# Moving 156 DMA issues of a hybrid encoder block from the sync queue to GpSimd's queue

## The chip, the cores and the metric

The kernel runs on one core of one Trainium2 chip. The core has five instruction streams that run side by side, each in its own order: TensorE (PE, with its weight loads as PEld), VectorE (DVE), ScalarE (ACT), GpSimd (POOL) and SyncE (SP). They wait for one another by semaphores. A DMA is an instruction on the stream that issues it; it waits there for its operands, and what stands behind it on that stream waits too. The metric is the device time of one execution in microseconds (us); lower is better.

## The reference, cut to what matters

One layer over 1040 tokens (16 meta tokens and 1024 frames) of width 1024, all in float32:

```
h = h + token_mixer(rmsnorm(h))          # proj = u @ w_in ; 4 mLSTM heads and 4 retention heads
h = h + channel_mixer(rmsnorm(h))        # (silu(conv(u @ w_up)) * (u @ w_gate)) @ w_down
return rmsnorm(h)[meta tokens dropped]

token_mixer:   q, k, v, gates = split(proj)
               h_head = chunkwise recurrence(q, k, v)          # per head
               mixed  = sigmoid or silu(gate) * head_norm(h_head)
               return mixed @ w_out
```

`mixed` has 2048 features: 8 heads of 256. `w_out` is 2048 x 1024, `w_down` is 2816 x 1024.

## The kernel before, in words

Activations lie transposed, features on the 128 partitions and tokens along the free axis. Each fp32 product is made of three products of halves (`hi` and `lo` of both sides), so each weight tile is loaded raw (`raw_*`, two buffers of a ring in all), then split: `hi` by ACT (L142) and `lo` by DVE (L143).

The token mixer goes head by head, h = 0 to 7. In a head, PE makes the gate projection `po` (L376 to L378) between the first chunks of the recurrence, then the value projection `pv` of the next head (L366 to L368) between the later chunks, then q and k of the next head (`pq`, `pk`). DVE evacuates `pq` and `pk` from three PSUM banks: L397 for mLSTM heads, L407 to L410 for retention heads. The finished features of a head, `mixed`, are made by DVE in tiles `mx` (L896, two buffers) and stored to DRAM, `mxd` (L908): six stores a head for heads 0 to 6, 42 in all. Head 7 stays on the chip.

The products with `w_out` and `w_down` come later and use a scheme of seven products in place of eight, which needs sums and differences of blocks of these weights. They are made ahead of time, one `wsum` at a time, in the evacuations of q and k: 8 for `w_out` (`wsw`) and 11 for `w_down` (`wsd`), 19 in all. One `wsum` loads two tiles of 128 x 1024 (L182, L183), combines them in place by four DVE instructions (L185 to L188) and stores four halves of 128 x 512 (L190). There is one buffer for each of its two tiles (`rr0`, `rr1`), so the loads of the next `wsum` wait until the stores of the last have landed. Three `wsum` stand in each of six heads and one in another. So twelve of them follow another in the same head.

Two more parts matter here. `last_two` (L169, L172) loads rows of `w_out` into the same ring of raw tiles, and DVE adds them into `acc` when a head's last piece of `mixed` is there; the raw tile is free after that, and the next head's `raw_v` goes into it. `tables` (L520, L521) loads rows of the gates, spread over all partitions, into `A1` and `A2`.

The order of each engine's instructions is set when the kernel is built, by a scheduler that simulates the program with costs of its own; DMA issues count there too. So an edit of a queue moves instructions on other engines as well. Before, SP issues all DMAs but one of ACT's, and POOL does little but memsets.

Of the kernel before, what the change touches and what calls it, by code (L numbers as in the profile page):

```python
# [30 lines left out]
HB = 4 * P  # L31
# [30 lines left out]
def body(ctx, tc, h_in, vecs, cst, mask_in, rot, w_v0, w_v, w_fm, w_out, w_up, w_gate, w_down, out):  # L62
    nc = tc.nc
# [9 lines left out]
    def after(later, first):  # L73

        tc.add_manual_dep(later.ins, first.ins.name, mybir.DependencyInfo(mybir.DependencyClass.NoSync, mybir.DependencyReason.DATA),
                          reason="order")
# [17 lines left out]
    mxd = [dram.tile([P, SEQ], F32, name=f"mxd{i}") for i in range(16)]  # L94
# [82 lines left out]
    sums = {(g, st, k): dram.tile([P, 2 * HB], F32, name=f"ws{g}{st}_{k}") for g, n in (("w", 8), ("d", KD)) for st in ("65", "73") for k in range(n)}  # L177

    def wsum(g, k):
        src, n = (w_out, 8) if g == "w" else (w_down, KD)  # L180
        a, b = (accp.tile([P, 2 * HB], F32, tag=f"rr{i}", name=f"ws{g}{k}_{i}") for i in range(2))
        nc.sync.dma_start(a, src[k])  # L182
        nc.sync.dma_start(b, src[k + n])  # L183
        w11, w21, w12, w22 = a[:, :HB], a[:, HB:], b[:, :HB], b[:, HB:]
        after(nc.vector.tensor_tensor(w22, w21, w22, ALU.add), last["qk"])  # L185
        nc.vector.tensor_tensor(w21, w21, w11, ALU.subtract)
        nc.vector.tensor_tensor(w11, w22, w11, ALU.subtract)
        nc.vector.tensor_tensor(w12, w12, w11, ALU.subtract)  # L188
        for st, i, x in (("65", 0, w11), ("65", 1, w22), ("73", 0, w12), ("73", 1, w21)):
            nc.sync.dma_start(sums[g, st, k][:, i * HB:(i + 1) * HB], x)  # L190

    wsums = [(g, k) for g, n in (("w", 8), ("d", KD)) for k in range(n)]

# [74 lines left out]
    def gained(kb, t0, t1, gcol, dve=False):  # L268
        g = vec[:, gcol + kb:gcol + kb + 1]
        if dve:  # L270
            nc.vector.tensor_scalar(uh[kb][:, t0:t1], resid[:, kb, t0:t1], g, None, ALU.mult)
        else:
            nc.scalar.activation(uh[kb][:, t0:t1], resid[:, kb, t0:t1], AF.Copy, scale=g)
        return nc.vector.scalar_tensor_tensor(ul[kb][:, t0:t1], resid[:, kb, t0:t1], g, uh[kb][:, t0:t1].bitcast(F32), ALU.mult, ALU.subtract)
# [33 lines left out]
    st = mix.enter_context(tc.tile_pool(name="st", bufs=1))  # L308
# [6 lines left out]
    def sig(b, p):  # L315
        t0, t1, _ = PIECES[p]
        return sigs[1][:, b] if p == 2 else sigs[0][:, b, max(t0, KEEP) - KEEP:t1 - KEEP]
# [387 lines left out]
    MA, MB = KEEP, KEEP + HALF  # L705
    wslots = {}

    def wact(q, k):
        i = ("A1", "B1", "B2", "A2").index(q) * 2 + k // 4
        if i not in wslots:  # L710
            wslots[i] = upool.tile([P, 2 * T], F32, tag=f"u{'hl'[i % 2]}{i // 2}", name=f"wa{i}")
        x = wslots[i][:, k % 4 * HB:(k % 4 + 1) * HB]
        mixw.act[q, k] = x
        return x
# [145 lines left out]
    def post_steps(h, p):  # L860
        t0, t1, chs = PIECES[p]
        n = len(chs)
        m = {}

        def stats():
            num, mv, base = outs.pop(p)
            z = mxp.tile([P, 4], F32, tag="z", name=f"z{h}_{p}", bufs=2)
            if h < H:
                den = base[:, 0:n, DV]
                e2 = cols[:, 2].rearrange("p (c h) -> p h c", h=H)[:, h, chs[0]:chs[0] + n]  # L870
                nc.vector.tensor_tensor(z[:, :n], den, den, ALU.mult)
                nc.vector.tensor_tensor(z[:, :n], z[:, :n], e2, ALU.max)
                nc.vector.scalar_tensor_tensor(z[:, :n], z[:, :n], EPS, mv[:, 0:n, 1], ALU.mult, ALU.add)
                nc.scalar.activation(z[:, :n], z[:, :n], AF.Sqrt)
            else:
                nc.scalar.activation(z[:, :n], mv[:, 0:n, 1], AF.Sqrt, bias=cs[:, C_EPS + h - H:C_EPS + h - H + 1])
            nc.vector.reciprocal(z[:, :n], z[:, :n])
            nc.vector.scalar_tensor_tensor(mv[:, 0:n, 1], mv[:, 0:n, 0], -1.0, z[:, :n], ALU.mult, ALU.mult)
            for i, c in enumerate(chs):
                L = CH[c][1]  # L880
                nc.scalar.activation(num[i][:L, :DV], num[i][:L, :DV], AF.Identity, bias=mv[:L, i, 1:2], scale=z[:L, i:i + 1])
            m["num"] = num

        def half(b):
            num = m["num"]
            tr = ps.tile([P, 512], F32, tag="tr", name=f"tr{h}_{p}_{b}")
            for i, c in enumerate(chs):
                c0, L = CH[c]
                nc.tensor.transpose(tr[:, c0 - t0:c0 - t0 + L], num[i][:L, b * P:(b + 1) * P], ident[:L, :L])
            a0 = max(t0, KEEP)  # L890
            w = t1 - a0
            g = (V_MLG if h < H else V_RTG) + (h % H) * 2 + b
            i = 2 * h + b

            def mix_into(dst, x0, x1):
                nc.vector.scalar_tensor_tensor(dst, tr[:, x0 - t0:x1 - t0], vec[:, g:g + 1], sig(b, p)[:, x0 - a0:x1 - a0], ALU.mult, ALU.mult)  # L896
            if h == 7:
                for q, o in (("A2", MA), ("B2", MB)):
                    x0, x1 = max(a0, o), min(t1, o + HB)
                    if x0 < x1:  # L900
                        mix_into(wact(q, 6 + b)[:, x0 - o:x1 - o], x0, x1)
                if t1 > MB + HB:
                    mix_into(mm[:, i], MB + HB, t1)
                return
            mx = mxp.tile([P, WMAX], F32, tag="mx", name=f"mx{h}_{p}_{b}", bufs=2)
            mix_into(mx[:, :w], a0, t1)
            e = min(t1, MB + HB)
            nc.sync.dma_start(mxd[i][:, a0 - MA:e - MA], mx[:, :e - a0])  # L908
            if e < t1:
                nc.vector.tensor_copy(mm[:, i], mx[:, e - a0:w])  # L910
        return [stats, lambda: half(0), lambda: half(1)]

    def ab(h, c):
# [47 lines left out]
    for i, (t0, t1) in enumerate(NP):  # L961
        for kb in range(KB):
            x = gained(kb, t0, t1, V_MIX, dve=kb < 4 if i == 0 else i > 1 and kb % 4 == 0)
# [19 lines left out]
    for h in range(8):  # L983
        A = lambda c, h=h: (lambda: scan_a(h, c))
        B = lambda c, h=h: ab(h, c)
        merge([lambda b=b, p=p: o_group(h, b, p) for b in range(2) for p in range(3)],
              [A(0)] + [B(c) for c in range(4 if h < 7 else NCH)])
        if h == 7:
            break
        side = post_steps(h, 0) + [B(4), B(5), B(6)] + post_steps(h, 1) + [B(7), B(8)] + post_steps(h, 2)  # L990
        merge([lambda c=c: v_group(h + 1, c)() for c in range(NCH)], side)
        tables(h + 1)
        for kind in "qk":
            for p in range(3):
                qk_group(h + 1, kind, p)
                if (kind, p) in (("q", 0), ("q", 2), ("k", 1)) and wsums:
                    wsum(*wsums.pop(0))
# [141 lines left out]
    for t, (st, k) in enumerate(mixw.steps):  # L1139
# [4 lines left out]
        if st == "65" and k == 1:  # L1144
            x = fp.tile([P, 4 * XW], F32, name="wm", tag="xh2", bufs=1)
# [175 lines left out]
    def up_part(i):  # L1321
        chunks = UC
        def done(m, half, c):
            if isinstance(c, list):
                t = ftile(f"c{i}_{m}{half}")
                for x, (j0, j1) in zip(c, chunks):
                    nc.scalar.copy(t[:, j0:j1], x)
                c = t
            conv(i, m, half, c)
        return seven("up", i, chunks, done)  # L1330

    def gate_part(i):
        def done(m, half, c):
            gate(i, m, half, c[0] if isinstance(c, list) else c[:, :HALF])
        return seven("ga", i, [(2, XW)], done)
# [50 lines left out]
    for i in range(1, NPAIR):  # L1386
        u, g = up_part(i), gate_part(i)
# [100 lines left out]
    for p in (1, 2):  # L1488
# [5 lines left out]
        else:  # L1494
            for mb in (1, 4):
                x = resid[:, mb, OP[2][0]:OP[2][1]]
# [84 lines left out]
```

## Time and profile before

| | us |
|---|---|
| median of 3 runs (1546.46 to 1555.4) | 1554.75 |
| the profiled execution, its own time | 1551.87 |
| its span | 1550.1 |
| PE busy in the span | 1515.9 |
| DVE busy in the span | 1123.7 |

The span runs from the first to the last instruction. A busy share is an average over stages; which wait ends last in a stage is read from the rows of that stage. A bracket at the end of a row of the timeline is the idle time of the engine ahead of that row and who ended it. "issue" there means that the engine waited for nothing that the profile shows. SPq is SP's queue of DMA issues, and the time of an SPq row is that of the issue, not of the transfer. Of the median's three runs one was at 1546.46 and one at 1555.4; the profiled execution lies between.

### The profile page before, as it was taken

Reading aid. Unit: us, or ns where it says so; the run is one execution under the profiler, and the core shown is the slowest. Engines: PE = TensorE matmul, PEld = TensorE weight load, DVE = VectorE, ACT = ScalarE, POOL = GpSimd, SP = SyncE. Lnnn points to the kernel's source line nnn. Section 1 sums busy time; section 2 is a strip of 40 time slices with the busy share of each in tenths; the row PEclk is TensorE's granted clock in tenths of the full one; section 3 lists DMA queues with packets and bytes.
Section 4 is the critical chain, followed back from the end, with each engine's and each line's share of the span. In section 5 each row is a group of like instructions: output and inputs, shape, how many; then the busy total and the mean of one; then the engine's idle time right before and its main releaser. Section 6 shows DMA issues by size and latency. Waiting matters only on the chain.

```text
span 1550.1 us, 25404 instructions
## 1 busy us (share of the span) xinstructions
PE 1515.9 (98%) x9753; PEld 1392.7 (90%) x9753; DVE 1123.7 (72%) x2387; ACT 737.0 (48%) x1493; POOL 2.4 (0%) x12
## 2 busy tenths in 40 slices
PE   7999999999999999999999999999999999999997
PEld 7989999999999999997788998999999999888887
DVE  8757768596767767679967778676666666778657
ACT  8574655545242433436454455444444444434443
POOL 0000000000000000000000000000000000000000
PEclk9999999999999999999999999999999999999999
DMA  6125435262534435227543235332222224933313
GB/s 214 42 70 168 158 106 182 86 225 96 179 116 149 146 116 171 88 84 250 177 137 108 82 96 177 102 98 87 82 82 79 79 82 148 374 98 114 95 41 109
DMA packets 92441, 197.41 MB, mean 127 GB/s; under 512 B 9048, under 2 KB 31264, under 8 KB 92320
## 3 DMA queue, kind: packets, MB, share of 16 engines
q1 hardware_dynamic: 92176, 195.73, 38.2%
q8 instruction: 76, 1.25, 0.3%
q14 instruction: 45, 0.37, 0.1%
q10 hardware_dynamic: 144, 0.07, 0.0%
HBM read 146.44 MB, written 49.32 MB: 126 GB/s over the span
## 4 chain that ended last, share of the span: by engine, by line
PE 85%; DMA 7%; DVE 4%; ACT 2%; issue 2%; SPq 0%; DVEq 0%; ACTq 0%
PE pv L366 4%; PE pv L367 4%; PE pv L368 3%; PE pdx L546 3%; PE pdx L548 3%; PE pdx L547 3%; PE po L378 3%; PE po L376 3%; PE po L377 3%; PE pup_x L547 2%; PE pup_x L548 2%; PE pga_x L546 2%; PE pup_x L546 2%; PE pga_x L548 2%; PE pga_x L547 2%; DMA A<-scr 2%
## 5 line engine op out<-in xcount | busy, mean ns | idle before, releaser
L366 PE MATMUL pv<-hi_v,uh 128*128 128x256 f32 (+1 forms) x512 | 146.5, 287 | 12.4 <-ACT hi_v L142 8.1
L367 PE MATMUL pv<-lo_v,uh 128*128 128x256 f32 (+1 forms) x512 | 145.7, 285 | 0.0
L368 PE MATMUL pv<-hi_v,ul 128*128 128x256 f32 (+1 forms) x512 | 144.9, 284 | 0.0
L376 PE MATMUL po<-uh,hi_o 128*128 128x386 f32 (+2 forms) x384 | 125.1, 326 | 0.0
L377 PE MATMUL po<-ul,hi_o 128*128 128x386 f32 (+2 forms) x384 | 123.3, 321 | 0.0
L378 PE MATMUL po<-uh,lo_o 128*128 128x386 f32 (+2 forms) x384 | 122.9, 320 | 0.0
L366 PEld LDWEIGHTS pv<-hi_v,uh 128*128 128x128 f32 x512 | 97.1, 190 | 15.9 <-ACT hi_v L142 8.1
L367 PEld LDWEIGHTS pv<-lo_v,uh 128*128 128x128 f32 x512 | 96.8, 189 | 0.9 <-DVE lo_v L143 0.8
L368 PEld LDWEIGHTS pv<-hi_v,ul 128*128 128x128 f32 x512 | 96.7, 189 | 0.1
L235 ACT CAST hi_up<-raw_up 128x512 fp32r<-128x512 f32 (+1 forms) x52 | 36.5, 720 | 108.5 <-PE pga_z L547 61.2
L376 PEld LDWEIGHTS po<-uh,hi_o 128*128 128x128 f32 x384 | 72.5, 189 | 0.2
L377 PEld LDWEIGHTS po<-ul,hi_o 128*128 128x128 f32 x384 | 72.4, 188 | 0.2
L378 PEld LDWEIGHTS po<-uh,lo_o 128*128 128x128 f32 x384 | 72.3, 188 | 0.1
L236 DVE TENSOR_TENSOR lo_ga<-fraw_ga,hi_ga 128x512 fp32r<-128x512 f32 (+1 forms) x52 | 41.8, 808 | 37.0 <-ACT hi_ga L235 36.9
L546 PE MATMUL pup_x<-uh_g,hi_up 128*128 128x256 f32 (+1 forms) x240 | 67.3, 283 | 1.2 <-ACT uh_g L1014 1.2
L547 PE MATMUL pup_x<-ul_g,hi_up 128*128 128x256 f32 (+1 forms) x240 | 67.5, 283 | 0.1
L236 DVE TENSOR_TENSOR lo_up<-raw_up,hi_up 128x512 fp32r<-128x512 f32 (+1 forms) x52 | 41.2, 809 | 35.0 <-ACT hi_up L235 34.2
L548 PE MATMUL pup_x<-uh_g,lo_up 128*128 128x256 f32 (+1 forms) x240 | 66.3, 282 | 0.0
L376 PE MATMUL pq<-uh,hi_q 128*128 128x400 f32 (+2 forms) x192 | 63.1, 328 | 1.7 <-DVE vl L342 1.6
L376 PE MATMUL pk<-uh,hi_k 128*128 128x400 f32 (+2 forms) x192 | 62.3, 324 | 2.0 <-DVE kT L409 1.5
L236 DVE TENSOR_TENSOR lo_d<-rd,hi_d 128x1024 fp32r<-128x1024 f32 (+1 forms) x34 | 37.6, 1112 | 34.0 <-ACT hi_d L235 34.0
L377 PE MATMUL pq<-ul,hi_q 128*128 128x400 f32 (+2 forms) x192 | 62.1, 323 | 0.0
(744 smaller groups left out, 4981.6 us busy)
## 6 DMA issues: line engine op xcount, KB each, us to landing
wsd<-w_down_d SPq DMA_DIRECT2D x22, 512.0 KB, 4.1
wsd<-wsd SPq DMA_DIRECT2D x44, 256.0 KB, 2.1
raw_up<-w_up_d SPq DMA_DIRECT2D x22, 512.0 KB, 3.6
fraw_ga<-w_gate_d SPq DMA_DIRECT2D x22, 512.0 KB, 3.6
acts<-cv SPq DMA_DIRECT2D x44, 256.0 KB, 2.0
rd<-wsd SPq DMA_DIRECT2D x22, 512.0 KB, 3.4
wsw<-w_out_d SPq DMA_DIRECT2D x16, 512.0 KB, 4.3
raw_o<-w_fm_d SPq DMA_DIRECT2D x16, 512.0 KB, 3.5
```

Source lines behind the costliest of these rows:

```text
L235: nc.scalar.copy(hi[:, o:o + n], x)
L236: nc.vector.tensor_tensor(lo[:, o:o + n], x, hi[:, o:o + n].bitcast(F32), ALU.subtract)
L366: nc.tensor.matmul(pv[:L, :nv], a, hi[:, o:o + nv], start=kb == 0, stop=False)
L367: nc.tensor.matmul(pv[:L, :nv], a, lo[:, o:o + nv], start=False, stop=False)
L368: nc.tensor.matmul(pv[:L, :nv], b, hi[:, o:o + nv], start=False, stop=kb == KB - 1)
L376: nc.tensor.matmul(pt[:, :n], a, uh[kb][:, t0:t1], start=kb == 0, stop=False)
L377: nc.tensor.matmul(pt[:, :n], a, ul[kb][:, t0:t1], start=False, stop=False)
L378: nc.tensor.matmul(pt[:, :n], b, uh[kb][:, t0:t1], start=False, stop=kb == KB - 1)
L546: m.append(nc.tensor.matmul(pt, ah, xh_, start=first and k == 0, stop=False, skip_group_check=True))
L547: nc.tensor.matmul(pt, ah, xl_, start=False, stop=False, skip_group_check=True)
L548: m.append(nc.tensor.matmul(pt, al, xh_, start=False, stop=last and k == n - 1, skip_group_check=True))
```

## The change

The two loads and four stores of each `wsum`, and the stores of `mx`, are issued from GpSimd's queue in place of SP's. SP keeps the loads of weights and tables, and the transfers of the later stages. That is 19 x 6 + 42 = 156 DMAs: SP has 348 rows in place of 504, POOL 172 in place of 16.

```
@@ wsum
-        nc.sync.dma_start(a, src[k])
-        nc.sync.dma_start(b, src[k + n])
+        nc.gpsimd.dma_start(a, src[k])
+        nc.gpsimd.dma_start(b, src[k + n])
...
         for st, i, x in (("65", 0, w11), ("65", 1, w22), ("73", 0, w12), ("73", 1, w21)):
-            nc.sync.dma_start(sums[g, st, k][:, i * HB:(i + 1) * HB], x)
+            nc.gpsimd.dma_start(sums[g, st, k][:, i * HB:(i + 1) * HB], x)
@@ post_steps, half
-            nc.sync.dma_start(mxd[i][:, a0 - MA:e - MA], mx[:, :e - a0])
+            nc.gpsimd.dma_start(mxd[i][:, a0 - MA:e - MA], mx[:, :e - a0])
```

SP's queue at the start of the program, before (`resid` is the input, `raw_q` and `raw_k` the first head's weights):

```order
L937 DMA resid<-h_in_d 128x8x384
L937 DMA resid<-h_in_d 128x8x256
L182 DMA wsw_0_1802<-w_out_d 128x1024
L183 DMA wsw_1_1803<-w_out_d 128x1024
L139 DMA raw_q_0_223<-w_fm_d 128x1024
L139 DMA raw_k_0_618<-w_fm_d 128x1024
```

and POOL's queue at the start, now:

```order
L332 MEMSET vh 128x258
L333 MEMSET vl 128x258
L182 DMA wsw_0_1802<-w_out_d 128x1024
L183 DMA wsw_1_1803<-w_out_d 128x1024
L334 MEMSET vh 128x9x2
L335 MEMSET vl 128x9x2
L336 MEMSET vh 128x9
L908 DMA mxd_94<-mx_0_0_1325 128x386
```

The first pair of `wsum` loads stood behind all loads of the input; it stands now behind two memsets at the very start and waits for nothing there.

DVE at the evacuation of k of head 4, with the second `wsum` of that stretch (`wsd_1_5191`, `wsd_0_5190`); one piece of the difference, `-` before, `+` now:

```order
-L185 TENSOR_TENSOR wsd_1_5191<-wsd_0_5190,wsd_1_5191 128x512
 L858 BN_AGGR mv_2_4962<-bn_7_4981 128x2
 L831 MEMSET mv_0_5426 128x2
-L186 TENSOR_TENSOR wsd_0_5190<-wsd_0_5190 128x512
 L407 TENSOR_TENSOR rk_0_5233<-pk_0_5208,A_173 64x400
 L408 TENSOR_TENSOR rk_0_5233<-pk_0_5208,A_173 64x400
 L409 TENSOR_TENSOR kT<-pk_0_5208,A_172 128x400
-L187 TENSOR_TENSOR wsd_0_5190<-wsd_1_5191,wsd_0_5190 128x512
 L342 SCALAR_TENSOR_TENSOR vl<-pv_8_5031,Rg,vh 128x256
 L774 TENSOR_TENSOR qd_2l<-qT,qd_2h 128x128
```

The evacuation of the first bank of k (L407 to L409) no longer stands behind L185, which waits for the two loads; L185 stands now twelve rows on, behind L410 of that bank.

SP's queue where head 1 ends and the weights of head 2 are loaded, now:

```order
L139 DMA raw_o_1_1894<-w_fm_d 128x1024
L169 DMA raw_m_2014<-w_out_d 128x1024
L169 DMA raw_m_2153<-w_out_d 128x1024
L520 DMA A_172<-scr 128x16
L139 DMA raw_v_0_2358<-w_v_d 128x1024
L139 DMA raw_v_1_2364<-w_v_d 128x1024
L139 DMA raw_q_0_2370<-w_fm_d 128x1024
```

Before, 22 DMAs of `wsum` and `mx` stood between the first and the last of these rows, and `raw_v` stood right behind a pair of `wsum` loads.

## Rows read from the trace of the kernel before

**Rows 1.** The page: busy time, share and instructions of each engine.
```profile
PE 1515.9 (98%) x9753; PEld 1392.7 (90%) x9753; DVE 1123.7 (72%) x2387; ACT 737.0 (48%) x1493; POOL 2.4 (0%) x12
```

**Rows 2.** The page: shares by engine of the chain that ended last.
```profile
PE 85%; DMA 7%; DVE 4%; ACT 2%; issue 2%; SPq 0%; DVEq 0%; ACTq 0%
```

**Rows 3.** Windows: stretch, busy time per engine, granted clock, DMA share, GB/s.
```profile
0.00:50.00 50.00, 41.54 (x301) 39.19 (x302) 41.56 (x112) 34.49 (x83) 1.03 (x10) 1.00 0.54 187
50.00:200.00 150.00, 144.39 (x1043) 139.33 (x1042) 108.01 (x322) 93.63 (x192) 0.00 (x0) 1.00 0.33 106
200.00:450.00 250.00, 243.51 (x1748) 235.02 (x1747) 187.22 (x490) 115.91 (x257) 0.00 (x0) 1.00 0.46 149
450.00:700.00 250.00, 250.00 (x1840) 246.39 (x1840) 178.53 (x445) 100.53 (x245) 0.00 (x0) 1.00 0.38 123
2.00:20.00 18.00, 11.87 (x84) 10.32 (x85) 15.28 (x41) 14.21 (x38) 0.00 (x0) 1.00 1.05 370
```

**Rows 4.** Timeline of SP's queue at the start: start, issue time, operation, count.
```profile
0.74 0.99 SPq L103 DMA_DIRECT2D resid<-h_in_d  x2
1.78 1.92 SPq L139 DMA_DIRECT2D raw_v<-w_v_d  x4
...
9.27 2.97 SPq L182 DMA_DIRECT2D wsw<-w_out_d  x1
12.28 0.44 SPq L183 DMA_DIRECT2D wsw<-w_out_d  x1
```

**Rows 5.** Timeline of PE: its first row, and one in head 4.
```profile
8.13 0.59 PE L366 MATMUL pv<-hi_v,uh 128*128 128x264 f32 x1 [8.13 <-ACT hi_v L142]
...
413.09 0.39 PE L376 MATMUL pk<-uh,hi_k 128*128 128x256 f32 x1 [1.51 <-DVE kT L409]
```

**Rows 6.** Timeline of DVE ahead of that row of head 4.
```profile
409.84 0.69 DVE L185 TENSOR_TENSOR wsd<-wsd,wsd 128x512 f32<-128x512 f32 x1 [3.92 <-issue]
...
411.29 0.58 DVE L407 TENSOR_TENSOR rk<-pk,A 64x400 f32<-64x400 f32 x1
411.88 0.57 DVE L408 TENSOR_TENSOR rk<-pk,A 64x400 f32<-64x400 f32 x1
412.46 0.57 DVE L409 TENSOR_TENSOR kT<-pk,A 128x400 f32<-128x400 f32 x1
...
414.54 0.57 DVE L410 TENSOR_TENSOR kT<-kT,rk 128x400 f32<-128x400 f32 x1
```

**Rows 7.** The chain in order of time, from one wsum of head 2 to the next.
```profile
227.85 0.69 DVE wsw L188
228.56 2.16 DMA wsw<-wsw
230.74 5.17 DMA wsw<-w_out_d
236.10 0.64 DVE wsw L185
```

**Rows 8.** DVE by line: busy us, mean ns, idle before and what ended it.
```profile
L185 DVE TENSOR_TENSOR wsd<-wsd,wsd 128x512 f32<-128x512 f32 x11 | 7.6, 687 | 11.7 <-issue 6.6 <-DMA wsd<-w_down_d 5.1
L185 DVE TENSOR_TENSOR wsw<-wsw,wsw 128x512 f32<-128x512 f32 x8 | 5.5, 686 | 4.2 <-DMA wsw<-w_out_d 2.9 <-issue 1.2
L400 DVE TENSOR_SCALAR cvq<-rq,vec 128x400 f32<-128x400 f32 (+2 forms) x12 | 4.8, 397 | 0.1
```

**Rows 9.** The chain in order of time, where head 3's raw_v is loaded.
```profile
254.85 1.28 DVE acc L172
```

**Rows 10.** Timeline of SP's queue at the same place.
```profile
254.40 0.33 SPq L182 DMA_DIRECT2D wsw<-w_out_d  x1
256.04 0.33 SPq L183 DMA_DIRECT2D wsw<-w_out_d  x1
256.42 0.42 SPq L139 DMA_DIRECT2D raw_v<-w_v_d  x1
```

**Rows 11.** Timeline of POOL: the memset ahead of the first DMA now, and its only arithmetic.
```profile
1.02 0.31 POOL L333 MEMSET vl<- 128x258 f32 x1
...
1544.02 1.41 POOL L1473 TENSOR_TENSOR resid<-resid,Rb 128x256 f32<-128x256 f32 x2 [1542.46 <-ACT Rb L304]
```

## The prediction, made before the changed kernel was timed

> **What bounds the kernel now.** I read the page's busy shares first. PE is busy for 1515.9 of 1550.1 us [rows 1], so all its idle time is 34 us, and no edit of queues can give back more than a part of that. The chain that ended last says the same: 85% PE, 7% DMA [rows 2]. Next I read the windows, to see where PE is idle [rows 3]. In the first 50 us it misses 8.5 us, in 50 to 200 it misses 5.6, in 200 to 450 it misses 6.5, and in 450 to 700 nothing, though the same three sums of weights are made there in each head. The edit touches 0 to 700 only. The granted clock is 1.00 in all these stretches, so the clock has no part in this.
>
> Two places show what the edit can move. At the start PE waits 8.13 us for the first split weights [rows 5], which stand behind the loads of `resid` and `raw_v` [rows 4]; from 2 to 20 us the DMA engines are full (share 1.05, 370 GB/s) [rows 3]. In the heads, DVE stops at L185, which opens each sum and waits for the two loads: 11.7 + 4.2 = 15.9 us in all [rows 8]. One case is in the rows: DVE stands still for 3.92 us at 409.84 [rows 6], the evacuation of k behind it is late, and PE waits 1.51 us for it at 413.09 [rows 5]. The chain goes through this ring too: the last store lands 2.16 us after its issue and the next pair of loads 5.17 us later [rows 7].
>
> **The change, part by part.** The sum is made against the profiled execution, 1551.87 us, which is 2.9 below the median of the runs and inside their spread.
>
> *The first pair of loads, +2.5 us.* Before, they are issued at 9.27 and 12.28, behind all input loads [rows 4]. Now they stand behind a memset that ends at 1.33 [rows 11], wait for nothing, and so compete with what PE's start needs: 0.59 MB of `resid` and 1.08 MB of `raw_v`. Together those take 1.67 / 0.370 = 4.5 us from 2 us on. The new pair is 1.05 MB, 2.8 us of full engines. The upper bound is 2.8, if all of it goes ahead of or between the needed loads; the lower is 0, if POOL issues it so late that they have landed. If it joins at about 3 us, some 1.3 MB of the needed loads are still to come, more than it has itself, so with equal shares nearly all of the 2.8 is lost; I take 2.5. PE is busy without a gap from 8.13 to 20 (11.87 us of 18) [rows 3], so there is no cover that takes it back. POOL's first DMA may be slower than later ones; that helps here.
>
> *The time of an issue on POOL.* The trace has none. The lower bound is SP's own issue, 0.33 us [rows 10]; the upper is SP's worst, 2.97 us on full engines [rows 4]. The nearest row of POOL itself is its tensor instruction, 1.41 us for two, 0.70 each [rows 11]. I take 0.70, because it is POOL's own time for work on 128 partitions, and keep 0.33 and 2.97 for the range.
>
> *The ring of the sums.* From the end of one L188 (228.54) to the next L185 (236.10) are 7.6 us [rows 7]. Two issues lie on that path in series, the last store and the second load, which waits for that store. So on POOL the ring takes 7.6 + 2 x (0.70 - 0.33) = 8.3 us, at 2.97 it takes 12.9. Against this the new order gives DVE more to do in between. In the excerpt of head 4 L407 to L410 come ahead of L185: 0.58 + 0.57 + 0.57 + 0.57 = 2.3 us [rows 6], beside three shorter instructions. Summed in the same way over the twelve sums that follow another in a head (rows of the order by their mean durations in the list of lines), the work between grows from 5.7 to 6.9 us, an estimate. DVE waits 15.9 / 12 = 1.3 us at each today, so it will wait 1.3 + 0.7 - 1.2 = 0.8, in all 9.6 in place of 15.9: 6.3 us less of DVE's standing still. PE lost 6.5 us in 200 to 450 while DVE lost up to 15.9, so at most 0.4 of a DVE wait reaches PE: **-2.5 us**.
>
> *What SP's freed queue is worth by itself, -1 us.* The next `raw_v` is issued at 256.42, right behind the pair of sums at 254.40 and 256.04 [rows 10], which looks like a queue in the way. But its buffer is held by DVE's L172 until 254.85 + 1.28 = 256.13 [rows 9]. So SP's queue costs it 0.3 us there, and the buffer sets the rest. Only where the new order takes L172 ahead of a sum does `raw_v` come earlier. In 200 to 450 I give that 1 us of the 6.5; the bounds are 0 and the 4 that the other terms leave.
>
> *Stores of `mixed`, 0.* Their results are read in the stage after 700; their two `mx` buffers are written again a piece later. If a store stood behind a sum's store for several us, the next L896 would wait, and DVE with it; that belongs to the POOL rival. The later loads of the sums, too, come long after the last store.
>
> *Issuing on another queue as such.* The rows show SP's issues at 0.33 us each, and 15.9 us of DVE waits that come from landing times. The Trainium skill, DMA: Bandwidth & Descriptors, section "Issuing engines are not separate DMA queues", says that several issuing engines only save the issue time on the sequencer, since all run on the same 16 DMA engines. By that the heads gain nothing and the sum is 1551.87 + 2.5 = 1554.4; by the rows it is 3.5 less, because of the order on DVE.
>
> The sum: 1551.87 + 2.5 - 2.5 - 1.0 = 1550.9, so **1551 us**. All three terms are below what three runs can tell (the runs of before differ by 9 us; about 1%, 15.5 us, is what a measurement of this kernel can tell from no change).
>
> **The rivals.**
>
> *POOL is slow (chance 0.18).* At 2.97 us an issue the ring takes 12.9 us, DVE waits 1.3 + 5.3 - 1.2 = 5.4 us at each of twelve sums, 65 in all, 49 more than now. At 0.4 of it on PE that is +20: 1551.87 + 2.5 + 20 = 1574. It decides from about 0.8 us an issue, where the lost and the gained parts balance, and costs over 1% from some 2.4 us. For it: POOL's own work is slower than DVE's (0.70 us for 128 x 256), its queue is in order, and six DMAs of a sum and the `mx` stores stand on it one behind another. Against: 0.70 is far from 2.97, which SP had only on full engines, and in 450 to 700 PE has shown that it loses nothing to sums.
>
> *The shared port (0.09).* DVE's one-source L400 takes 397 ns at mean for up to 400 elements, 12 for q [rows 8] and as many for k, three quarters of them in heads with sums; if it kept POOL from working while it ran, two issues of a ring could each be late by up to 0.42 us, so 12 x 0.84 = 10 us of DVE waits and 4 on PE: 1551 + 4 = 1555. The Trainium skill, SBUF — State Buffer, section "SBUF: two separate sides", states this rule: a DMA issued from GpSimd has its descriptors written by GpSimd, which is locked out while DVE runs a copy-like instruction on both ports. No row of this trace shows it, for POOL issues nothing here.
>
> *The waits were covered anyway (0.13).* Only the start term is left, as a different order moves PE's small waits about: 1554.
>
> *PE's idle time in 50 to 700 goes away (0.12).* 5.6 + 6.5 = 12.1 us [rows 3], and the start costs nothing: 1540. For it: the chain has DMA in it exactly there. Against: much of that idle time ends with DVE's own work or with `A` tables, whose load waits for their buffer.
>
> **How the numbers follow.** My forecast, 1551, has 0.48; its own range is 1546 to 1556. Slower by over 1% (above 1570) is the upper two thirds of the POOL case, 0.12, and I add 0.01 for a stall of `mx`: 0.13. Faster by over 1% (below 1539) needs nearly all idle time of the heads, about half of its rival: 0.07. The rest, 0.80, is within 1%. For 8 in 10 the range takes the forecast, the covered case, the port, most of the idle case and the milder POOL cases: 1541 to 1568.
>
> **What would show it.** Right: PE's first row at about 10.6 in place of 8.13; the bandwidth of the first 8 us unchanged; L185 with about 10 us of idle time ahead of it in place of 15.9; the 1.51 us wait in head 4 gone; POOL's issues under 1 us each. Wrong: PE starting at 8 (the first term falls), idle time ahead of L185 of 30 us or more, with PE waiting for evacuations of q and k (POOL is slow), or a POOL queue that is solid with issues. If PE's windows of 450 to 700 drop below 250, the sums have become a bound where they were not.

## The result, and the profile after

The changed kernel takes 1559.49 us (median of 15 runs, 1555.01 to 1563.57); the kernel before, beside it, 1553.27 (15 runs). The ratio is 1.0037, 95% interval [1.0026, 1.0048]. So it is slower by 6 us, where I had forecast 1551. The time lies in my range and within the 1% that I called no change, but on the wrong side: the interval excludes both my gain and no change. All ratios here leave out two runs far above the rest at a lower granted clock, one of firstsync_late_restgps (2971.02 us at 0.976) and one of before beside it (1645.55 us at 0.849). The profiled execution took 1560.63 us with a span of 1558.8, 8.7 more than the span of before.

The page after, its row of busy times, which answers to [rows 1]:

```profile
PE 1520.6 (98%) x9753; PEld 1395.6 (90%) x9753; DVE 1125.0 (72%) x2387; ACT 736.9 (47%) x1493; POOL 87.5 (6%) x168
```

POOL's new busy time is its 156 issues. The work of the others is the same to half a per cent. The windows, with the columns of [rows 3]:

```profile
0.00:50.00 50.00, 39.31 (x279) 36.27 (x280) 39.27 (x103) 32.76 (x80) 2.33 (x12) 1.00 0.54 187
50.00:200.00 150.00, 142.65 (x1011) 137.26 (x1010) 106.86 (x315) 91.28 (x181) 13.15 (x24) 0.99 0.33 106
200.00:450.00 250.00, 244.94 (x1766) 237.90 (x1768) 187.40 (x494) 118.83 (x266) 39.13 (x72) 1.00 0.46 146
450.00:700.00 250.00, 250.00 (x1836) 245.04 (x1828) 178.90 (x442) 96.61 (x239) 31.48 (x58) 1.00 0.37 123
2.00:20.00 18.00, 11.47 (x75) 9.22 (x76) 11.87 (x33) 10.93 (x31) 0.89 (x5) 1.00 1.06 373
```

PE misses 2.2 us more in the first 50 and 1.7 more in 50 to 200; in 200 to 450 it regains 1.4. The windows are cut by time. Laid at PE's own rows, its idle time is 2.6 us above that of before at the end of the first head's q, and 2.5 above at the end of the last head's k. Not all of the span's 8.7 us is waiting: PE is busy for 4.7 us more (1520.6 against 1515.9), and the granted clock of 50 to 200 is 0.99 in place of 1.00. The DMA engines are as full at the start as before (373 GB/s against 370). The start, POOL first, then PE where the first matmul stands and where q begins (start, duration, engine, line, operation, in brackets the idle time ahead):

```profile
1.36 0.71 POOL L182 DMA_DIRECT2D wsw<-w_out_d  x1
2.07 0.54 POOL L183 DMA_DIRECT2D wsw<-w_out_d  x1
...
8.53 0.59 PE L366 MATMUL pv<-hi_v,uh 128*128 128x264 f32 x1 [8.53 <-ACT hi_v L142]
...
40.02 0.45 PE L376 MATMUL pq<-uh,hi_q 128*128 128x400 f32 x1 [1.50 <-DVE gts L344]
```

POOL issues a DMA in 0.54 us, the first in 0.71. PE starts at 8.53, 0.40 later than in [rows 5] and not 2.5. Yet q begins 2.7 us later than before (its row of before, at 37.30, follows with the experiments), behind a wait for DVE's `gts`. DVE at L185, the same two rows as in [rows 8]:

```profile
L185 DVE TENSOR_TENSOR wsd<-wsd,wsd 128x512 f32<-128x512 f32 x11 | 7.6, 687 | 14.2 <-DMA wsd<-w_down_d 9.4 <-issue 4.8
L185 DVE TENSOR_TENSOR wsw<-wsw,wsw 128x512 f32<-128x512 f32 x8 | 5.5, 686 | 5.0 <-issue 4.1 <-DMA wsw<-w_out_d 0.9
```

That is 19.2 us of standing still, more than the 15.9 of before; I had forecast 9.6. The place in head 4 that I had picked does what I said, though. DVE after, beside [rows 6]:

```profile
414.78 0.57 DVE L410 TENSOR_TENSOR kT<-kT,rk 128x400 f32<-128x400 f32 x1
...
417.24 0.69 DVE L185 TENSOR_TENSOR wsd<-wsd,wsd 128x512 f32<-128x512 f32 x1 [1.76 <-DMA wsd<-w_down_d]
```

L185 stands behind the evacuation of k, its wait is 1.76 in place of 3.92, and PE's 1.51 us for `kT` are gone.

### The profile page after: what moved, and what is told of

It reads as the page before. It is cut to its first block, busy times and chain, and to the rows that moved or that the text cites. A ratio compares the mean times of both kernels' runs of the same rounds, so it can differ in the third digit from the quotient of the medians.

```text
span 1558.8 us, 25449 instructions
## 1 busy us (share of the span) xinstructions
PE 1520.6 (98%) x9753; PEld 1395.6 (90%) x9753; DVE 1125.0 (72%) x2387; ACT 736.9 (47%) x1493; POOL 87.5 (6%) x168
## 4 chain that ended last, share of the span: by engine, by line
PE 82%; DMA 7%; DVE 5%; issue 3%; ACT 2%; POOL 0%; DVEq 0%; SPq 0%; POOLq 0%; ACTq 0%
PE pv L366 4%; PE pv L367 4%; PE pv L368 3%; PE pdx L546 3%; PE pdx L548 3%; PE pdx L547 3%; PE pup_x L547 2%; PE pup_x L548 2%; PE pup_x L546 2%; PE pga_x L546 2%; PE pga_x L548 2%; PE pga_x L547 2%; DMA A<-scr 2%; PE po L378 2%; PE po L376 2%
## 5 line engine op out<-in xcount | busy, mean ns | idle before, releaser
L378 PE MATMUL pq<-uh,lo_q 128*128 128x400 f32 (+2 forms) x192 | 62.0, 323 | 0.0
```

The lines of the kernel that those rows point to most:

```text
L378: nc.tensor.matmul(pt[:, :n], b, uh[kb][:, t0:t1], start=False, stop=kb == KB - 1)
```

## The experiments

The queue and the order change together here: the scheduler (the "planner" of some expectations) orders PE, ACT and DVE anew for each choice of queues. So most kernels below hold one of the two fixed. The program is built once with queues `ORDER_OF` and the order of PE, ACT and DVE is read from it; it is built again with queues `QUEUES`, and dependencies that set order alone, without a wait, hold each of the three engines to the order read. Its core:

```
+    first, _ = build(ORDER_OF, None)
+    for i in first.all_instructions():
+        if i.engine in (E.PE, E.Activation, E.DVE):
+            plan.setdefault(i.engine, []).append(i.name)
+    nc, arrays = build(QUEUES, plan)          # in it, for neighbours p, q of a plan:
+        tc.add_manual_dep(q, p.name, <order only>)
-        nc.sync.dma_start(a, src[k])
+        Q["ld"](nc).dma_start(a, src[k])      # and so with b, the stores and mxd
```

All ratios are against the kernel before, run beside on the same chip, in five rounds, with 95% intervals. "Idle" is DVE's idle time ahead of L185; "PE idle" is the span less PE's busy time, both of the profiled run. The traces bear the orders out: in each pair that is said to share an order, all rows of PE, DVE and ACT stand in the same order (in oldorder_mxgps two rows of DVE are exchanged).

### Order and queue apart

`QUEUES` all GpSimd, `ORDER_OF` all sync:

> PE, ACT and DVE run in exactly the order of the kernel before, but the loads and stores of sums and the stores of mixed go through GpSimd's queue as in the changed kernel. Theory start: what costs is the early first pair of sum loads, about 3.4 us at the start whatever the order, and the rest of the queues is neutral: 1553.3 + 3.4 = 1556.7, ratio 1.002. Rival order: the queues cost nothing, the 6 us come from the new order of PE, ACT and DVE: ratio 1.000. Rival queue: everything comes from the queues, ratio 1.004, as the changed kernel's.

The other way round:

> The other corner: PE, ACT and DVE run in exactly the order of the changed kernel, but all transfers are issued from the sync queue as before. Theory start: the first 3.4 us are not lost (pq's first row within 1 us of before's), and what the new order costs by itself is left, 2 to 3 us: ratio 1.0015. Rival order: 1.004, the whole loss. Rival queue: 1.000.

Old order, only the first two loads on GpSimd, and all but these:

> Old order of PE, ACT and DVE, and only the two loads of the first sum go through GpSimd. Theory start: the two loads take DMA time from resid and raw_v, the first row of pq is 2.7 us later as in the changed kernel, and all 3.4 us stay to the end: ratio 1.002. Rivals order and queue in the heads: the start has cover, or the loss is made up in the heads, ratio 1.000.

> Old order of PE, ACT and DVE, and everything the change moves goes through GpSimd except the first two loads of a sum, which stay on the sync queue. Theory start: no loss at the start, so 1.000, and the idle time of DVE ahead of L185 shrinks a little by the freed sync queue (under 2 us, ratio 0.999 to 1.000). Rival queue: the issues on GpSimd in the heads cost, 1.002 to 1.004.

| order | queues | ratio | idle, us | PE idle, us |
|---|---|---|---|---|
| old | sync (before) | 1 | 15.9 | 34.2 |
| old | GpSimd, oldorder_allgps | 1.0106 [1.0084, 1.0129] | 32.0 | 45.4 |
| old | GpSimd but the first pair, oldorder_restgps | 1.0097 [1.0070, 1.0124] | 34.2 | 44.1 |
| old | the first pair on GpSimd, oldorder_firstgps | 1.0015 [0.9999, 1.0030] | 13.8 | 35.9 |
| new | sync, neworder_allsync | 0.9998 [0.9980, 1.0016] | 7.0 | 33.0 |
| new | GpSimd (after) | 1.0037 [1.0026, 1.0048] | 19.2 | 38.2 |

No theory had this. The queues cost 16 us under the old order and 6 under the new one, and the new order hides part of that cost. What I then held to be the cause, the early pair, is not it: PE's row at which q begins, in before, in oldorder_firstgps, and in neworder_allsync, where the pair is issued on the sync queue at 9.20 as before:

```profile
37.30 0.34 PE L376 MATMUL pq<-uh,hi_q 128*128 128x400 f32 x1
```
```profile
37.63 0.34 PE L376 MATMUL pq<-uh,hi_q 128*128 128x400 f32 x1
```
```profile
39.73 0.45 PE L376 MATMUL pq<-uh,hi_q 128*128 128x400 f32 x1 [1.50 <-DVE gts L344]
```

The early pair costs 0.3 us (1.1 in oldorder_allgps). The new order costs 2.4 without it, by the same wait for `gts` as in the changed kernel: the scheduler had set the first rows otherwise. In the new order DVE's L143 for k, which waits 1.36 us for ACT, stands at 37.46, ahead of the two L344 that make `gts` (the second at 39.99); before, the second L344 stood at 36.46 and L143 behind it at 37.19.

With equal orders the traces can be laid one on another. The second sum of head 2, in oldorder_restgps on POOL and DVE:

```profile
230.89 0.54 POOL L190 DMA_DIRECT2D wsw<-wsw  x1 [0.60 <-DVE wsw L188]
...
233.90 0.55 POOL L183 DMA_DIRECT2D wsw<-w_out_d  x1 [0.65 <-DMA wsw<-wsw]
...
239.35 0.69 DVE L185 TENSOR_TENSOR wsw<-wsw,wsw 128x512 f32<-128x512 f32 x1 [2.23 <-DMA wsw<-w_out_d]
```

and the same load on SP in the kernel before, where L188 ended at 228.53 and the store was issued at 228.56 [rows 7]:

```profile
230.74 0.33 SPq L183 DMA_DIRECT2D wsw<-w_out_d  x1
```

From the store's issue to the second load's issue are 3.01 us on POOL and 2.18 on SP. Where this comes from shows in the chain that ended last, here in the changed kernel from a store to the load behind it:

```profile
337.05 2.29 DMA wsw<-wsw
...
339.37 0.63 issue
340.00 4.63 DMA wsd<-w_down_d
```

The store has landed at 339.34, and the load that waits for it is issued 0.66 us later; before, that step took 0.02 us (a store lands at 230.72, the load is issued at 230.74 [rows 7]). From the last store's landing to the second load's issue the median of the twelve sums is 0.68 us in oldorder_allgps; in oldorder_storesgps (below), with the loads on SP, it is 0.05 to 0.07 at all twelve. In the mean over the twelve sums that follow another in a head, worked out from their rows:

| us | L188's end to last store's issue | to second load's issue | to L185 | ring |
|---|---|---|---|---|
| before | 0.12 | 2.33 | 4.95 | 7.39 |
| oldorder_allgps | 0.41 | 3.34 | 4.99 | 8.74 |
| after | 0.41 | 3.44 | 5.43 | 9.28 |

The ring is longer by 1.35 us under the old order, 12 x 1.35 = 16.2, and the idle time grew by 32.0 - 15.9 = 16.1. (The row of the changed kernel has the new order too; with this order on sync, in neworder_allsync, the ring is 8.32.) PE's waits in oldorder_allgps (total, times, longest):

```profile
PE tr L889 <- DVE mx L896: 7.1, 7, 2.2
...
PE pk L376 <- DVE kT L409: 3.2, 1, 3.2
```

Before, these rows had 1.2 and 1.5 us. In the old order L896 and L409 stand behind L185 in these places, so PE waits with DVE. Its idle time grew by 11.2 us in all (34.2 to 45.4), against DVE's 16.1; its busy time grew by 2.9 besides (1518.8 against 1515.9).

### Which transfers

Old order, with the loads of sums, their stores, or the stores of `mixed` alone on GpSimd:

> Old order of PE, ACT and DVE; all loads of sums (the first pair too) go through GpSimd, their stores and the stores of mixed stay on the sync queue. Theory ring: with everything on GpSimd each sum that follows another in a head came 1.0 to 1.5 us later (from the end of L188 to the next L185), because every hand-over DVE to store, store to load, load to DVE takes longer there; the loads have about half of it: DVE waits of some 25 us ahead of L185 (before 15.9, all on GpSimd 32 to 34), ratio 1.005. Rival mixed: the stores of mixed are what hurts on GpSimd's queue, 1.000 to 1.0015 here.

> Old order of PE, ACT and DVE; only the four stores of each sum go through GpSimd, all loads and the stores of mixed stay on the sync queue. Theory ring: the other half of the longer ring, the hand-over from DVE to the store (0.41 us in place of 0.03) and the issue (0.54 in place of 0.32): DVE waits of some 24 us ahead of L185, ratio 1.005, and no loss in the first 50 us. Rival mixed: 1.000.

> Old order of PE, ACT and DVE; only the stores of mixed go through GpSimd. Theory ring: they are in no ring, 1.000. Rival: their hand-over from DVE is also late and holds the two mx buffers and with them L896 and PE's transposes, ratio 1.002, so that loads (1.0043), stores (1.0036) and these make up the whole 1.0106.

Loads 1.0043 [1.0028, 1.0059], idle 21.2, ring 7.85; stores 1.0036 [1.0021, 1.0051], idle 24.5, ring 8.12; `mixed` 1.0006 [0.9991, 1.0021], idle 10.9, ring 6.99. So loads and stores of the sums each carry about 0.4 per cent and `mixed` nothing that can be told, as the ring has it. In the last, DVE waits 5.0 us less than before and no gain in time shows: what a wait of DVE costs isn't in proportion to its length.

### Taking the waits away

First the sums were moved in the program: one in the v stage, one behind q, one in the o stage (`one_sum` makes the next one in line).

```
-                if (kind, p) in (("q", 0), ("q", 2), ("k", 1)) and wsums:
+                if (kind, p) in (("q", 1),) and wsums:
-        side = post_steps(h, 0) + [B(4), B(5), B(6)] + ...
+        side = post_steps(h, 0) + [B(4), B(5), one_sum, B(6)] + ...
-              [A(0)] + [B(c) for c in range(4 if h < 7 else NCH)])
+              [A(0)] + [B(c) for c in range(2)] + [one_sum] * (0 < h < 7) + [B(c) for c in range(2, 4 if h < 7 else NCH)])
```

> The changed kernel's queues, but a head's three sums are no longer made one behind another while q and k are computed: one stands in the middle of the v stage, one behind the second piece of q, one in the middle of the o stage. Theory ring: a sum that follows 10 us or more behind the last one finds its loads landed, so the idle time ahead of L185 falls from 19 to under 6 us and the kernel is no slower than before, ratio 0.995 to 1.000. Rival queue as such: GpSimd's issues cost wherever they stand, 1.003 to 1.006. A different order may cost a little at the start, as the changed kernel's did (3 us).

> The same three places for the sums, with all transfers on the sync queue as in the kernel before. Theory ring: idle time ahead of L185 under 4 us in place of 15.9, ratio 0.995 to 0.999, and the difference to its sister with GpSimd's queues is under 0.2 per cent. Rival: the sums' waits never reached PE, or the sums disturb the v and o stages as much, ratio 1.000 to 1.003.

With GpSimd 1.0053 [1.0038, 1.0069], idle 18.1; with sync 0.9993 [0.9983, 1.0003], idle 7.8. The expectation fell, but its condition was hardly met either: in the built kernels a head's three sums still follow one another closely. From one L188 to the next L185 are 7.0 to 10.9 us in spread_sync and 8.0 to 12.1 in spread_gps, against 6.6 to 9.9 before. So these two don't test what sums far apart would do; they show that L185 still stands where its loads have not landed. The clock has a part too: in spread_sync the granted clock of 50 to 200 us is 0.95, against 1.00 before, and its twelve runs list 0.991 to 0.993 for the whole, where those of before have 0.995 in the mean. By the 1.0 us for each 0.001 worked out at the end of this text that is some 3 us, an estimate, which hide what else the places gave. (Each of the two kernels has an order of its own, so their difference isn't the queue alone.)

So the place of L185 itself was moved, in the order read from the first build:

```
+    for k in range(len(SUMS) - 1, -1, -1):    # SUMS[k]: L185 to L188 of sum k; DOWN = 10
+        for name in reversed(SUMS[k]):
+            p = seq.index(name)
+            seq.insert(p + DOWN * (k % 3), seq.pop(p))
```

> All queues as in the changed kernel, the order of the kernel before, except that in each head the second sum's four DVE instructions stand 10 rows (about 5 us) and the third's 20 rows further down DVE's order. Theory ring: what GpSimd's queues cost is DVE standing still at L185, placed where the planner thinks that the loads have landed; with 5 us more work ahead of each L185 the 34 us of idle time there fall below 10 and the loss with them: ratio 0.998 to 1.002 in place of 1.0106. Rival queue as such (issues on GpSimd, descriptors, shared DMA engines slow other work wherever the sums stand): still 1.006 to 1.010.

> The same order (second sums 10, third sums 20 rows further down), all transfers on the sync queue. Theory ring: idle time ahead of L185 under 4 us in place of 15.9, and the part of it that reached PE before comes back: ratio 0.996 to 0.999, and within 0.2 per cent of its sister with GpSimd's queues. Rival: the waits of the kernel before were covered, 1.000 to 1.001.

late_allgps: 0.9994 [0.9981, 1.0006] in place of 1.0106; late_allsync: 0.9967 [0.9952, 0.9982]. L185 in late_allgps, and then PE's wait at the transposes:

```profile
L185 DVE TENSOR_TENSOR wsd<-wsd,wsd 128x512 f32<-128x512 f32 x11 | 7.5, 681 | 1.6 <-DMA wsd<-w_down_d 1.6
L185 DVE TENSOR_TENSOR wsw<-wsw,wsw 128x512 f32<-128x512 f32 x8 | 5.4, 681 | 0.2 <-issue 0.2
```
```profile
PE tr L889 <- DVE mx L896: 1.2, 2, 0.6
```

All 156 transfers are still on GpSimd; only rows of DVE moved, and 17 us went. The same move gives 5 us on the sync queue: late_allsync has 0.1 us of idle time and is 0.27 per cent faster than its sister, a little more than expected; the intervals touch at their ends. So of the queue's 16 us under this order about 4 are left where the waits are gone, and about 12 were the wait.

### The changed kernel's own order

Its ring alone taken away; its start alone, by these two lines against the changed kernel; both:

```
-        nc.gpsimd.dma_start(a, src[k])
-        nc.gpsimd.dma_start(b, src[k + n])
+        (nc.sync if (g, k) == ("w", 0) else nc.gpsimd).dma_start(a, src[k])
+        (nc.sync if (g, k) == ("w", 0) else nc.gpsimd).dma_start(b, src[k + n])
```

> The changed kernel's own order and queues, with the second sum of a head 10 and the third 20 rows further down DVE's order. Theory, two causes: the waits ahead of L185 (19.2 us) fall under 3 and give PE back 4 to 7 us; the 3.2 us that this order loses at the start stay: ratio 0.999 to 1.001 in place of 1.0037. Rival: in the changed kernel's own order the ring is not the cause, 1.003 to 1.004.

> The changed kernel with one difference: the first sum's two loads stay on the sync queue, and the planner orders the program anew. Theory, two causes: pq's first row comes within 0.6 us of before's in place of 2.7 later, the waits ahead of L185 stay near 19 us: ratio 1.0015. Rival: the start was made up for later anyway, 1.003 to 1.004.

> Both causes taken away while GpSimd keeps its transfers: the order that the planner makes with the first two loads on the sync queue, second sums 10 and third sums 20 rows further down DVE's order, all other sums and the stores of mixed on GpSimd. Theory, two causes: no loss at the start, waits ahead of L185 under 3 us, ratio 0.996 to 0.999. Rival: issues on GpSimd cost something of their own, 1.000 to 1.002.

| | ratio | idle, us | q begins, against before |
|---|---|---|---|
| after | 1.0037 [1.0026, 1.0048] | 19.2 | +2.7 |
| neworder_late_allgps | 1.0011 [0.9996, 1.0026] | 0.0 | +3.3 |
| firstsync_restgps | 1.0008 [0.9991, 1.0025] | 20.5 | -0.9 |
| firstsync_late_restgps | 0.9979 [0.9965, 0.9994] | 0.0 | -0.5 |

The ring has 0.26 of the changed kernel's loss, the start 0.29, and the two together 0.58 per cent: they add up. firstsync_restgps is ordered anew, but its order differs from that of the changed kernel in 132 of PE's 9753 places and 35 of DVE's 2387 only. With both gone a kernel that keeps all transfers but the first pair on GpSimd is 0.21 per cent faster than before.

### The versions that the findings point to

The order that the scheduler makes with the first pair on sync, run with all transfers on sync, as it is and with the sums late:

> The order that the planner makes when the first two loads of a sum stay on the sync queue and all else goes to GpSimd, run with all transfers on the sync queue. Theory: the 3 us that the changed kernel's order loses at the start (PE waits for gts at pq's first row) come from the planner's belief that the early loads compete, so they are gone here, and the heads keep the short waits at L185 (7 us): ratio 0.997 to 0.999. Rival: the start of an order is luck, 0.9995 to 1.001 as with the changed kernel's order on the sync queue.

> The best of both: the same order and the same later places, all transfers on the sync queue. Theory: the 8.2 us of waits ahead of L185 that are left in that order go too, and at 0.4 of them give PE 3 us: ratio 0.994 to 0.996. Rival: what is left is covered, 0.9967 as without the later places.

The first is 0.9967 [0.9957, 0.9978], as expected; the second 0.9998 [0.9981, 1.0014], a miss. Its idle time is 0.0 in place of 8.2 and its time is not better. In that order the 8.2 us were covered, or the late sums hold up something else; which, wasn't settled. The two were run on different chips, each beside its own runs of before.

neworder2_allsync has the order of firstsync_restgps, and neworder2_late_allsync that of firstsync_late_restgps. So there are five pairs that differ in the queues alone:

| order | GpSimd | sync | difference, per cent | idle, us |
|---|---|---|---|---|
| old | 1.0106 | 1 | +1.06 | 32.0 and 15.9 |
| changed kernel's | 1.0037 | 0.9998 | +0.39 | 19.2 and 7.0 |
| firstsync_restgps | 1.0008 | 0.9967 | +0.41 | 20.5 and 8.2 |
| old, sums late | 0.9994 | 0.9967 | +0.27 | 1.8 and 0.1 |
| firstsync_restgps, sums late | 0.9979 | 0.9998 | -0.19 | 0.0 and 0.0 |

(In the third and the last the first pair is on sync on both sides.) With the waits GpSimd's queue is slower in all three; without them it is slower in one pair and faster in the other, and there the intervals touch or overlap. So the best versions are late_allsync and neworder2_allsync, both 0.33 per cent under the kernel before and with no transfer on GpSimd.

## Why the prediction was wrong, step by step

- **The ring of the sums, the step that failed.** This is the term of -2.5. I priced a ring on POOL at two issues, 2 x 0.37 = 0.7 us, and set against it 1.2 us more of DVE work. The issue was even cheaper than I took (0.54 us, not 0.70; 0.33 on SP), so the two issues explain 0.4. The ring grew by 1.35. What I left out are the hand-overs: from L188's end to the store's issue 0.41 in place of 0.12, and from there to the second load's issue 1.0 more, of which only 0.2 is the store's own issue and some 0.65 lie between the store's landing and the load's issue. Why POOL takes longer at both is not shown. On the other side the new order took 8.9 us from DVE's idle time (15.9 to 7.0 on the sync queue), where I had counted 12 x 1.2 = 14.4, though seven of the twelve waits were shorter than 1.2 us and can't fall below nothing. The queue then gave 12.2 back. Sum: +3.3 of DVE's idle time in place of -6.3. On PE, from the end of the first head's q to the end of the last head's k, I had forecast -3.5 with SP's term; its idle time changed by -4.3 in neworder_allsync and by -0.1 in the changed kernel. So the new order gave what I had hoped for, and the queue took it back.
- **What of DVE's wait reaches PE.** I took 0.4 as an upper value, but set the 6.5 us of PE in 200 to 450 against DVE's waits in all heads. In 200 to 450 alone the waits at L185 are 10.9 us, so the bound should have been 0.6. By PE's idle time 5.2 of 12.2 us came through under the new order (0.4) and 11.2 of 16.1 under the old one (0.7). It isn't a constant; it hangs on what stands behind the wait.
- **The first pair of loads, +2.5.** The size was near (2.7 at the first row of q, 3.4 by q's end), the mechanism was wrong. Competing loads cost 0.3 to 1.1 us, not 2.5: PE's first row came at 8.53, not at 10.6. The rest is the order, DVE's L143 ahead of `gts`, which I had not laid side by side for the first 50 us. That the sum had this term right is luck.
- **SP's freed queue, -1.** Not shown: where the ring's waits are gone, GpSimd's version is slower by 0.27 per cent in one pair and faster by 0.19 in the other.
- **The clock, no part.** The runs give it one: 0.99 in 50 to 200 in the changed kernel's profiled run, against 1.00, is 1.5 us of 150, an estimate.
- **Stores of `mixed`, 0.** Right: 1.0006 [0.9991, 1.0021].
- **450 to 700.** Right: 250.00 of 250 busy, as before. The stall in head 4 went, as said.
- **The rivals.** "POOL is slow" had 0.18 and the right place: a ring that takes longer, DVE stopped in it, PE behind. Its price was wrong, since I had tied it to the issue alone: the balance was to tip at 0.8 us an issue, and it had tipped at 0.54. The shared port: in the changed kernel from L188's end to the last store's issue are 0.40 to 0.42 us at each of 19 sums, whatever DVE ran next (L400 at three of them), so no lockout behind single instructions of DVE shows there. The rule that GpSimd can't write descriptors while DVE runs a copy-like instruction (Trainium skill, SBUF — State Buffer, "SBUF: two separate sides") had no run of its own. By the Trainium skill's section "Issuing engines are not separate DMA queues" (DMA: Bandwidth & Descriptors) the heads gain nothing, and the sum was 1554.4; that was the better number. The measured 1559.5 lies above it, since the rule speaks of issue time on the sequencer, and here a chain of DMAs and engines that wait for one another paid at each hand-over (0.41 in place of 0.03 us, 0.68 in place of 0.05).

## What to carry to other kernels

A DMA in a ring (compute, store, load into the same buffer, compute) cost its hand-overs here more than its issue: before such a ring is moved to another queue, measure from the end of the last instruction to the start of the next, and look at what stands behind the waiting instruction. Where a scheduler sets the order, an edit of a queue is two edits: hold the order fixed and change the queue, then the other way round, before a cause is named. A wait that the scheduler underrates was cheaper to cure by putting the waiting instruction ten or twenty rows later than by another queue; in one order that gained nothing (neworder2_late_allsync), so it has to be measured each time.

## What the runs showed of the hardware that was not expected

- A DMA issue holds POOL for 0.54 us for 128 x 512 and 128 x 1024 alike, and SP for 0.33. A store that waits for DVE is issued 0.41 us after DVE's instruction ends on POOL and 0.03 on SP, where nothing else is in the way. A load that waits for a store of its own buffer is issued about 0.67 us after the store's landing on POOL (medians 0.67 and 0.68 in the changed kernel and in oldorder_allgps) and 0.02 to 0.07 on SP.
- Two loads of 0.5 MB each, issued at 1.36 and 2.07 on a second queue while the DMA engines were full (373 GB/s), delayed PE's first row by only 0.40 us. Over all traces it stands at 8.50 to 9.10 in the seven kernels with the early pair and at 7.56 to 8.43 in the eleven others, 0.8 apart in the mean.
- The runs of one kernel differ by up to 11 us (those of before, beside the first four, by 15), and they line up with the granted clock that each run lists, a mean over the run between the two levels (1.2 and 2.4 GHz) and close to the upper one. In neworder2_late_allsync 0.998 goes with 1546.79 us and 0.992 with 1554.0; over the 15 runs of the changed kernel a line through them falls by 1.0 us for each 0.001 of clock. So a ratio of 1.002 from a few runs can be the clock alone, an estimate from that line. The 6 to 15 runs behind each ratio here, beside 15 to 35 of before, bring the intervals to 0.1 to 0.3 per cent to either side.
